# A hybrid backbone layer on one core: the third branch projection in two parts, by K tiles, with its last operands kept in SBUF

## The chip, the cores and the metric

One core of a Trainium2 chip runs the whole kernel. The metric is the device time of one execution in microseconds (us); less is better. The profile and the trace come from one further execution, recorded by the hardware profiler.

## What is computed

One layer for 256 latent tokens, with 256 context tokens as a prefix, model width 2048, all in f32:

```python
h = rms_norm(x) * (1 + scale) + shift            # latent and context tokens
(na_q, na_k, na_v, na_gate, pool_u, pool_gate, rw_r, rw_k, rw_v, rw_gate, rw_lw, rw_la, merge_logits) = split(h @ w_in)
y_na   = neighbourhood_attention(...)            # 16 heads of 64
y_pool = multiscale_pool(...)                    # windows 2, 4, 8, 16
y_rw   = rwkv_readout(wkv_scan(...), ...)        # RWKV-7, two directions, 16 heads of 64, context first
b_na, b_pool, b_rw = y_na * silu(na_gate), y_pool * silu(pool_gate), y_rw * silu(rw_gate)      # 256 x 1024 each
g_na, g_pool, g_rw = split(sigmoid(merge_logits))                                           # 256 x 2048 each
merged = g_na * (b_na @ w_branch[0]) + g_pool * (b_pool @ w_branch[1]) + g_rw * (b_rw @ w_branch[2])
out = rms_norm(x + gate * (merged @ w_out)) * final_g
```

## The kernel before, in words

**Products.** Every large product is made of f32r halves: an operand x is kept as `hi` (rounded) and `lo = x - hi`, and three matmuls (`mm3`, L582 to L584) add hi*hi, hi*lo and lo*hi. Weights come as raw tiles of 512 KB (`load_unit`, L564, three buffers `raw`); `split_half` cuts each in two halves, with a cast on ScalarE (`whi`, L576) and a subtraction on VectorE (`wlo`, L577), into five buffers of each. A *unit* is one raw tile. `group` (a product of 256 tokens by 512 columns) takes one unit for two K tiles: 4 calls of `mm3`, 12 matmuls. Two PSUM accumulators `dg`, one for each half of the tokens, come from a pool of two, so the next group's first matmul on one of them waits until `done` has read the group before.

**Stages.** Up to about 140 us the adaLN factors and h are made. Then, to about 1280 us, the columns of w_in are projected, eight head pairs of attention and of RWKV and the pooling are worked off beside them, and the 12 groups of merge logits (16 K tiles each) go to DRAM as tanh (`md_`). From 1280 us come the *branch groups*: three branches of four column groups c, 8 K tiles each, so 4 units and 48 matmuls in a group. `branch_load` (L623) fetches the operands of two K tiles at a time from DRAM (`bs`), where `keep` (L842 to L846: a cast, a subtraction and two stores) put the hi and lo halves of each head pair. K tile k of branch 2 is RWKV head pair k. `gates_in` (L923) loads a group's gates from `md_` into two buffers `mt`, which stand ahead of the last unit; `done` (L928, L930) makes (gate + 1) * accumulator on VectorE and, from branch 1 on, adds it to `sums`. After branch 2's group c, `turned` (L639 to L646) transposes the sums on TensorE and writes their hi and lo halves for w_out. From about 1479 us w_out is multiplied (L1211, L1212 split its weights).

**RWKV.** `rwkv(p)` runs for head pairs 0 to 7: features, scores, `inverse` (31 steps on VectorE and two trips through DRAM, L299 to L321), `merge`, a chain of 8 steps (`px` L374, `py` L382, `pu` L388, `pS` L398, `py` L411, each 8 small matmuls, with VectorE, ScalarE and GpSimd between them), the readout (`pm`, `pvv`, L108, L109), and `keep(2, p, g)`, after which the event `rw<p>` is marked.

**Order.** `Order` is a planner that runs when the kernel is built. It has a clock of its own (0.68 us for an `mm3` of 512 columns, given figures for the bursts of attention and RWKV and for the waits after them), and it writes TensorE's order out by hand: ready bursts of the streams go in between units. `units()` is the stream of units: first `todo`, then `late`, the twelve branch groups. A group of branch 2 is only taken when the event `rw7` lies behind on the planner's clock; three half units are taken ahead. `branch_load` 8 to 11 (branch 2's operands) too stand behind `rw7` there. From `side7` (the last attention) on, every second half unit also calls `gate_piece`: a 256 KB load `wg` (L1069) into one of the two buffers `kt`, and a VectorE instruction `gs` (L1072, L1074) that adds it up. There are 64 of these; after every 16th, `gate_out` makes a matmul `pg` and a store. All loads are issued by SyncE's queue (SP), in one order fixed at build time by the framework's scheduler, which also orders the other engines' instructions; each queue works in that order and waits where it has to. Behind the loop, SP loads x, the gate and final_g for the end (L1200, 16 loads of 256 KB).

Of the kernel before, what the change touches and what calls it, by code (L numbers as in the profile page):

```python
# [9 lines left out]
F32 = mybir.dt.float32  # L10
# [506 lines left out]
NT = 256  # L517
# [12 lines left out]
def hybrid_block(ctx, tc, x, cx, w_ms, w_st, w_in, w_mg, w_br, w_out, pool_w, icnt, wa, bias, rows, params, out, dbg=None):  # L530
# [80 lines left out]

    def branch_st(br):
        def st(k):
            c = slice(256 * (k % 2), 256 * (k % 2) + 256)
            return hh[4 * br + k // 2][:, c], hl[4 * br + k // 2][:, c]
        return st

    def branch_load(i):

        br, k = i // 4, 2 * (i % 4)  # L620
        for e, y in enumerate((hh, hl)):
            x = y[i] = hp.tile([P, 512], F32R, tag=f"h{'hl'[e]}{i}", name=f"b{'hl'[e]}{i}")
            nc.sync.dma_start(x.bitcast(F32).rearrange("p (k t) -> p k t", k=2), bs[2 * br + e][k // 2].rearrange("k p t -> p k t"))  # L623

    def branch_src(br, c):
        return lambda u: w_br[br, 4 * c:4 * c + 4, :, 256 * u:256 * u + 256].rearrange("n p c -> p n c")

    def merged(t, c):
# [3 lines left out]
        return sums[t, c]  # L632
    sums = {}
    mhl = {}
# [189 lines left out]
    with ExitStack() as mx:  # L824
# [6 lines left out]
        O = Order(tc)  # L831
        T = {}

# [82 lines left out]

        def branch_group(br, c):
            th = {}

            def gates_in(u):  # L920
                for t in range(2):
                    th[t] = wp.tile([P, 512], F32, tag="mt", bufs=2, name=f"bth{br}_{c}_{t}")
                    nc.sync.dma_start(th[t], md_[4 * br + c][t])  # L923
                return u()

            def done(t, a):
                o = merged(t, c) if br == 0 else th[t]
                nc.vector.scalar_tensor_tensor(o, th[t], 1.0, a, ALU.add, ALU.mult)  # L928
                if br:
                    nc.vector.tensor_tensor(merged(t, c), merged(t, c), o, ALU.add)  # L930
                if br == 2 and t and c < 3:
                    O.add(turn(c), 1)
            us = group(8, branch_src(br, c), branch_st(br), done)
            us[3] = lambda u=us[3]: gates_in(u)
            return us

        def turn(c):
            yield 0.0, 2.0
            for t in range(2):
                turned(c, t)  # L940
                yield 0.55, 0.2


        def rwkv(p):
# [32 lines left out]
            nc.vector.scalar_tensor_tensor(g, y, 0.5, g, ALU.mult, ALU.mult)  # L977
            keep(2, p, g)
            O.mark(f"rw{p}")

# [122 lines left out]
        for i in range(12):  # L1103
            todo.append((None, lambda i=i: merge_group(i)))
        late = [(br, c) for br in range(3) for c in range(4)]

        def units():
# [4 lines left out]
            while True:  # L1112
                while len(ready) < AHEAD:
                    if not halves:
                        if not cur:
# [3 lines left out]
                            if i is not None:  # L1119
                                cur = todo.pop(i)[1]()  # L1120
                                if not todo:
                                    last = 0
                            elif not todo and late and (late[0][0] < 2 or O.has("rw7")):
                                assert O.has("side7")
                                cur = branch_group(*late.pop(0))
                            else:
                                break
                        halves = cur.pop(0)()
                        if last is not None:
                            if last in (5, 6, 7, 8, 10, 12, 14, 16):  # L1130
                                branch_load(last - 5 if last < 9 else last // 2 - 1)
                            if last >= 18 and loads and O.has("rw7"):
                                branch_load(loads.pop(0))
                            last += 1
                    ready.append(halves.pop(0)())
                    n += 1
                    if n % 2 and O.has("side7") and gates:
                        gate_piece(*gates.pop(0))
# [144 lines left out]
```

## Time and profile before

| | us |
|---|---|
| median of 3 runs | 1576.07 (1574.93 to 1576.57) |
| the profiled execution, device time | 1578.95 |
| its span, first to last instruction | 1577.2 |
| TensorE matmul busy | 1498.5 (95%) |
| TensorE weight load | 1204.1 (76%) |
| VectorE busy | 1163.0 (74%) |
| ScalarE busy | 795.6 (50%) |
| GpSimd busy | 250.8 (16%) |

The mean granted TensorE clock is 0.985 of full speed. 289 MB move by DMA, 183 GB/s over the span. TensorE sets the length nearly everywhere; the stretch from 1275 to 1445 us is where its busy share falls.

### The profile page before, as it was taken

What the parts mean: (1) busy time and instruction counts of PE and PEld (TensorE: products, weight loads), DVE (VectorE), ACT (ScalarE), POOL (GpSimd) and SP (SyncE); (2) the same over time, 40 slices, a digit from 0 to 9 for tenths busy, and PEclk for the clock granted to TensorE, in tenths of its full rate; (3) what the DMA queues carried; (4) which work ended last, traced back from release to release, by engine and by line L of the source; (5) the groups of instructions that cost most, each with busy time, mean ns of one, the idle gap of its engine ahead of it and who ended that gap; (6) DMA issues with size and microseconds to landing.
All of it is one profiled execution on the core that took longest, in us unless ns stands there. A gap on an engine that the chain in (4) does not pass through costs nothing.

```text
span 1577.2 us, 31852 instructions
## 1 busy us (share of the span) xinstructions
PE 1498.5 (95%) x12024; PEld 1204.1 (76%) x12024; DVE 1163.0 (74%) x2630; ACT 795.6 (50%) x1593; POOL 250.8 (16%) x437
## 2 busy tenths in 40 slices
PE   6999989999999999999999999999999997987998
PEld 4667868788877897788789877877897775666887
DVE  4224787788788777886887778778779987886764
ACT  5224663566365546544664556446546542333553
POOL 2222010050023013200230230023023200120000
PEclk9999999999999999999999999999999999998999
DMA  9996435445543464343345533533566698987763
GB/s 373 343 334 229 144 128 173 145 155 176 162 142 105 131 179 142 102 131 121 98 158 153 174 96 119 165 122 113 176 191 211 209 311 246 296 261 259 242 208 112
DMA packets 210186, 289.23 MB, mean 183 GB/s; under 512 B 62576, under 2 KB 159984, under 8 KB 205424
## 3 DMA queue, kind: packets, MB, share of 16 engines
q1 hardware_dynamic: 203120, 277.76, 54.4%
q10 hardware_dynamic: 6912, 9.44, 1.7%
q8 instruction: 94, 1.54, 0.4%
q14 instruction: 60, 0.49, 0.1%
HBM read 265.38 MB, written 21.50 MB: 182 GB/s over the span
## 4 chain that ended last, share of the span: by engine, by line
PE 72%; DVE 10%; DMA 10%; ACT 3%; issue 3%; SPq 1%; ACTq 0%; POOL 0%; DVEq 0%; POOLq 0%
PE d L814 27%; PE dg L582 7%; PE dg L583 6%; PE dg L584 5%; DVE wlo L577 3%; PE acc L735 2%; PE psm L683 2%; PE o L582 2%; PE o L584 2%; PE o L583 2%; DMA raw<-in_w_br 2%; DMA raw<-in_w_in 2%; PE acc L738 2%; PE acc L741 2%; PE pu L388 1%
## 5 line engine op out<-in xcount | busy, mean ns | idle before, releaser
L576 ACT CAST whi<-raw 128x512 fp32r<-128x512 f32 x584 | 353.9, 619 | 397.7 <-PE d L814 158.9
L577 DVE TENSOR_TENSOR wlo<-raw,whi 128x512 fp32r<-128x512 f32 x584 | 401.4, 699 | 101.5 <-ACT whi L576 74.0
L814 PE MATMUL d<-hh,whi 128*128 128x256 f32 (+1 forms) x1184 | 366.4, 329 | 1.6 <-ACT mth L910 0.8
L814 PE MATMUL d<-hl,whi 128*128 128x256 f32 (+1 forms) x1184 | 357.8, 322 | 0.0
L814 PEld LDWEIGHTS d<-hh,whi 128*128 128x128 f32 x1184 | 224.8, 190 | 25.1 <-issue 2.9
L814 PE MATMUL d<-hh,wlo 128*128 128x256 f32 (+1 forms) x1184 | 241.2, 323 | 0.0
L814 PEld LDWEIGHTS d<-hl,whi 128*128 128x128 f32 x1184 | 225.2, 190 | 16.1 <-issue 0.2
L814 PEld LDWEIGHTS d<-hh,wlo 128*128 128x128 f32 x1184 | 182.4, 190 | 16.9 <-issue 0.7
L370 POOL TENSOR_SCALAR sg<-SV,G 64x64 f32<-64x64 f32 x192 | 112.4, 591 | 365.5 <-DVE SV L407 208.9
L582 PE MATMUL dg<-whi,hh 128*128 128x512 f32 x384 | 165.4, 431 | 4.9 <-DVE gnag L854 3.2
L583 PE MATMUL dg<-whi,hl 128*128 128x512 f32 x384 | 152.1, 396 | 0.0
L584 PE MATMUL dg<-wlo,hh 128*128 128x512 f32 x384 | 151.9, 396 | 0.1
L582 PE MATMUL dg<-whi,bh 128*128 128x512 f32 x192 | 82.7, 431 | 17.8 <-ACT whi L576 7.5
L582 PEld LDWEIGHTS dg<-whi,hh 128*128 128x128 f32 x384 | 73.0, 190 | 26.4 <-DVE gnag L854 4.6
L584 PEld LDWEIGHTS dg<-wlo,hh 128*128 128x128 f32 x384 | 73.0, 190 | 17.2 <-DVE wlo L577 0.6
L583 PEld LDWEIGHTS dg<-whi,hl 128*128 128x128 f32 x384 | 73.3, 191 | 10.5 <-issue 0.2
L584 PE MATMUL dg<-wlo,bh 128*128 128x512 f32 x192 | 78.4, 408 | 2.7 <-DVE wlo L577 2.7
L583 PE MATMUL dg<-whi,bl 128*128 128x512 f32 x192 | 78.0, 406 | 1.9 <-DMA bl<-bs 1.9
L309 DVE TENSOR_TENSOR iM<-iA,iT 128x126 f32<-128x126 f32 (+22 forms) x248 | 63.7, 257 | 17.1 <-DMA iA<-dA 10.8
L311 DVE TENSOR_TENSOR iT<-iT,iM 128x126 f32<-128x126 f32 (+22 forms) x248 | 62.8, 253 | 6.4
L748 ACT ACTIVATE hh<-xT,md 128x256 fp32r<-128x256 f32 x32 | 17.5, 594 | 89.3 <-DVE md L705 89.3
L582 PEld LDWEIGHTS dg<-whi,bh 128*128 128x128 f32 x192 | 37.6, 196 | 30.0 <-ACT whi L576 12.1
(320 smaller groups left out, 2510.1 us busy)
## 6 DMA issues: line engine op xcount, KB each, us to landing
raw<-in_w_in SPq DMA_DIRECT2D x244, 512.0 KB, 3.8
wm<-in_w_ms SPq DMA_DIRECT2D x32, 1024.0 KB, 6.9
raw<-in_w_br SPq DMA_DIRECT2D x48, 512.0 KB, 5.1
wg<-in_w_mg SPq DMA_DIRECT2D x64, 256.0 KB, 4.2
raw<-in_w_out SPq DMA_DIRECT2D x32, 512.0 KB, 4.2
wst<-in_w_st SPq DMA_DIRECT2D x16, 448.0 KB, 7.4
sl<-in_bias SPq DMA_DIRECT2D x32, 128.0 KB, 3.1
iA<-dA SPq DMA_DIRECT2D x16, 256.0 KB, 5.6
```

Source lines behind the costliest of these rows:

```text
L309: nc.vector.tensor_tensor(m, A[:, st:st + 1, st + 1:32].to_broadcast([128, ni, nt]), T[:, 0:ni, st:st + 1].to_broadcast([128, ni, nt]), AL ...
L311: nc.vector.tensor_tensor(T[:, 0:ni, st + 1:32], T[:, 0:ni, st + 1:32], m, ALU.add)
L370: nc.gpsimd.tensor_scalar(sg[hv[par], d], SV[hv[par], par, w, d], G[hv[par], gs[d][0], d:d + 1], None, ALU.mult)
L576: nc.scalar.copy(hi, src)
L577: nc.vector.tensor_tensor(lo, src, hi.bitcast(F32), ALU.subtract)
L582: nc.tensor.matmul(acc, a[0], b[0], start=start, stop=False)
L583: nc.tensor.matmul(acc, a[1], b[0], start=False, stop=False)
L584: nc.tensor.matmul(acc, a[0], b[1], start=False, stop=stop)
L683: mm = nc.tensor.matmul(psm[j][32 * g:32 * g + 32, 0:256], cs[:, kt], wm[:, k], start=(kt < 4), stop=(kt >= 12), tile_position=(0, 32 * g))
L735: mm = nc.tensor.matmul(acc[i], shi[:, c], hh[j], start=(j == 0), stop=False)
L738: nc.tensor.matmul(acc[i], slo[:, c], hh[j], start=False, stop=False)
L814: nc.tensor.matmul(box[0], w[m >= 8][:, 128 * i:128 * i + 128], x, start=(v == 0 and m == 0), stop=(v == 3 and m == 11))
```

## The change

The groups of branch 2 come in two parts. Part 1 of a column group takes K tiles 0 to 5 (3 units, 36 matmuls) and only needs the event `rw5`; part 2 takes K tiles 6 and 7 (1 unit, 12 matmuls) and needs `rw7`. All four groups of part 1 stand ahead of the four of part 2. Each part has its own gate multiplication and addition to `sums`; in part 2 the addition is on GpSimd for c = 0 to 2 and on VectorE for c = 3. The gates of part 2 are loaded a second time from `md_` (`ahead`), during part 1 for c = 0 to 2, into buffers `kt`, `sl` and `vT`, which `gate_piece` and `gate_out` used until then, and for c = 3 into the two buffers `mt`, with its unit. So that those buffers are free, a gate piece comes with two of three half units instead of one of two. Head pair 7 is not stored and loaded again: its two halves stay in SBUF (`T["last"]`). `branch_load` 8 to 11 need `rw6` instead of `rw7`, come with every second unit, and the last one loads only head pair 6. The planner waits 3.0 us instead of 2.0 before the transposes.

```diff
--- before.py
+++ after.py
@@ -609,8 +609,11 @@
             return [lambda h=h: half(h) for h in range(2)]
         return [lambda u=u: load(u) for u in range(nk // 2)]
 
-    def branch_st(br):
+    def branch_st(br, k0=0):
         def st(k):
+            k += k0
+            if br == 2 and k == 7:
+                return T["last"]
             c = slice(256 * (k % 2), 256 * (k % 2) + 256)
             return hh[4 * br + k // 2][:, c], hl[4 * br + k // 2][:, c]
         return st
@@ -620,17 +623,21 @@
         br, k = i // 4, 2 * (i % 4)
         for e, y in enumerate((hh, hl)):
             x = y[i] = hp.tile([P, 512], F32R, tag=f"h{'hl'[e]}{i}", name=f"b{'hl'[e]}{i}")
+            if i == 11:
+                nc.sync.dma_start(x[:, 0:NT].bitcast(F32), bs[2 * br + e][3][0])
+                continue
             nc.sync.dma_start(x.bitcast(F32).rearrange("p (k t) -> p k t", k=2), bs[2 * br + e][k // 2].rearrange("k p t -> p k t"))
 
-    def branch_src(br, c):
-        return lambda u: w_br[br, 4 * c:4 * c + 4, :, 256 * u:256 * u + 256].rearrange("n p c -> p n c")
+    def branch_src(br, c, u0=0):
+        return lambda u: w_br[br, 4 * c:4 * c + 4, :, 256 * (u + u0):256 * (u + u0) + 256].rearrange("n p c -> p n c")
 
     def merged(t, c):
 
         if (t, c) not in sums:
             sums[t, c] = hp.tile([P, 512], F32, tag=f"h{'hl'[t]}{12 + c}", name=f"sum{t}_{c}")
         return sums[t, c]
-    sums = {}
+    sums, T = {}, {}
+
     mhl = {}
 
     def turned(c, t):
@@ -829,7 +836,6 @@
         hps = cp.tile([P, 8], F32, name="hps")
         nc.vector.tensor_scalar(hps, pp[:, PC_PS:PC_PS + 8], 0.5, None, ALU.mult)
         O = Order(tc)
-        T = {}
 
         def ztile(tag, nm, n):
             z = zp.tile([P, n, 258], F32, tag=tag, bufs=1, name=nm)
@@ -914,7 +920,8 @@
             src = lambda u: w_in[MERGE + 4 * i:MERGE + 4 * i + 4, :, 256 * u:256 * u + 256].rearrange("n p c -> p n c")
             return group(16, src, lambda k: (hh[k][:, 256:512], hl[k][:, 256:512]), lambda t, d: merge_out(i, t, d))
 
-        def branch_group(br, c):
+        def branch_group(br, c, part=0):
+
             th = {}
 
             def gates_in(u):
@@ -923,19 +930,38 @@
                     nc.sync.dma_start(th[t], md_[4 * br + c][t])
                 return u()
 
+            def ahead(u):
+
+                for t in range(2):
+                    tag, n = (("kt", 2), ("sl", 3), (("sl", 3), ("vT", 1))[t], ("mt", 2))[c]
+                    pool = wp if tag == "mt" else np_
+                    x = gates2[c, t] = pool.tile([P, 512], F32, tag=tag, bufs=n, name=f"cth{c}_{t}")
+                    nc.sync.dma_start(x, md_[8 + c][t])
+                return u()
+
             def done(t, a):
-                o = merged(t, c) if br == 0 else th[t]
-                nc.vector.scalar_tensor_tensor(o, th[t], 1.0, a, ALU.add, ALU.mult)
+                g = gates2[c, t] if part == 2 else th[t]
+                o = merged(t, c) if br == 0 else g
+                nc.vector.scalar_tensor_tensor(o, g, 1.0, a, ALU.add, ALU.mult)
                 if br:
-                    nc.vector.tensor_tensor(merged(t, c), merged(t, c), o, ALU.add)
-                if br == 2 and t and c < 3:
+                    (nc.gpsimd if part == 2 and c < 3 else nc.vector).tensor_tensor(merged(t, c), merged(t, c), o, ALU.add)
+                if part == 2 and t and c < 3:
                     O.add(turn(c), 1)
-            us = group(8, branch_src(br, c), branch_st(br), done)
-            us[3] = lambda u=us[3]: gates_in(u)
+            if part == 2:
+                us = group(2, branch_src(br, c, 3), branch_st(br, 6), done)
+                if c == 3:
+                    us[0] = lambda u=us[0]: ahead(u)
+                return us
+            us = group(6 if part else 8, branch_src(br, c), branch_st(br), done)
+            us[-1] = lambda u=us[-1]: gates_in(u)
+            if part and c < 3:
+                us[1] = lambda u=us[1]: ahead(u)
             return us
 
+        gates2 = {}
+
         def turn(c):
-            yield 0.0, 2.0
+            yield 0.0, 3.0
             for t in range(2):
                 turned(c, t)
                 yield 0.55, 0.2
@@ -975,8 +1001,15 @@
             yield f"rwg{p}"
             g = T[f"rwg{p}"]
             nc.vector.scalar_tensor_tensor(g, y, 0.5, g, ALU.mult, ALU.mult)
-            keep(2, p, g)
-            O.mark(f"rw{p}")
+            if p < 7:
+                keep(2, p, g)
+            else:
+                h = wp.tile([P, NT], F32R, tag="th", bufs=1, name="lasth")
+                l = np_.tile([P, NT], F32R, tag="ql", name="lastl")
+                nc.scalar.copy(h, g)
+                nc.vector.tensor_tensor(l, g, h.bitcast(F32), ALU.subtract)
+                T["last"] = h, l
+            O.mark(f"rw{p}", 1.5 * (p == 7))
 
         def attention(p):
             yield f"nav{p}"
@@ -1102,7 +1135,7 @@
                     todo.append((f"at{p}", gate_(PL_G + p - 1 + e, f"plg{p - 1 + e}", "g2p", 2)))
         for i in range(12):
             todo.append((None, lambda i=i: merge_group(i)))
-        late = [(br, c) for br in range(3) for c in range(4)]
+        late = [(br, c) for br in range(2) for c in range(4)] + [(2, c, part) for part in (1, 2) for c in range(4)]
 
         def units():
             ready, halves, cur = [], [], []
@@ -1120,7 +1153,7 @@
                                 cur = todo.pop(i)[1]()
                                 if not todo:
                                     last = 0
-                            elif not todo and late and (late[0][0] < 2 or O.has("rw7")):
+                            elif not todo and late and (len(late[0]) < 3 or O.has(("rw5", "rw7")[late[0][2] - 1])):
                                 assert O.has("side7")
                                 cur = branch_group(*late.pop(0))
                             else:
@@ -1129,12 +1162,12 @@
                         if last is not None:
                             if last in (5, 6, 7, 8, 10, 12, 14, 16):
                                 branch_load(last - 5 if last < 9 else last // 2 - 1)
-                            if last >= 18 and loads and O.has("rw7"):
+                            if last >= 18 and last % 2 == 0 and loads and O.has("rw6"):
                                 branch_load(loads.pop(0))
                             last += 1
                     ready.append(halves.pop(0)())
                     n += 1
-                    if n % 2 and O.has("side7") and gates:
+                    if n % 3 and O.has("side7") and gates:
                         gate_piece(*gates.pop(0))
                 if not ready:
                     if not todo and not late:
```

## Rows read from the trace of the kernel before

**Rows 1.** Page, 40 slices of the span: TensorE's busy share, tenths.
```profile
PE   6999989999999999999999999999999997987998
```

**Rows 2.** Stretches: us, busy PE, PEld, DVE, ACT, POOL, PEclk, DMA share, GB/s.
```profile
1230.00:1240.00 10.00, 9.94 (x82) 7.41 (x82) 9.87 (x20) 7.70 (x21) 3.72 (x7) 1.00 0.51 158
...
1290.00:1300.00 10.00, 8.06 (x27) 5.89 (x26) 8.58 (x21) 2.35 (x5) 0.00 (x0) 0.83 1.03 351
...
1330.00:1340.00 10.00, 5.26 (x24) 4.06 (x23) 3.48 (x8) 0.83 (x2) 0.00 (x0) 1.00 0.66 176
...
1410.00:1420.00 10.00, 5.80 (x45) 4.08 (x42) 6.71 (x19) 3.24 (x6) 0.00 (x0) 0.59 0.55 179
...
1430.00:1440.00 10.00, 2.72 (x6) 1.86 (x7) 1.16 (x2) 0.00 (x0) 0.00 (x0) 0.62 0.93 306
...
1450.00:1460.00 10.00, 10.00 (x47) 7.95 (x47) 8.24 (x15) 5.04 (x10) 0.00 (x0) 1.00 1.00 342
```

**Rows 3.** Timeline of TensorE, 1407 to 1443 us: start, duration, instruction, [idle before].
```profile
1407.61 0.40 PE L584 MATMUL dg<-wlo,bh 128*128 128x512 f32 x1
...
1418.93 0.63 PE L582 MATMUL dg<-whi,bh 128*128 128x512 f32 x1
...
1428.15 0.39 PE L583 MATMUL dg<-whi,bl 128*128 128x512 f32 x1
1428.38 0.39 PE L584 MATMUL dg<-wlo,bh 128*128 128x512 f32 x1
1435.41 0.77 PE L582 MATMUL dg<-whi,bh 128*128 128x512 f32 x1 [6.64 <-DMA bh<-bs]
...
1442.77 0.39 PE L582 MATMUL dg<-whi,bh 128*128 128x512 f32 x1
```

**Rows 4.** Chain that ended last, 1428 to 1438 us: start, duration, what.
```profile
1428.17 3.41 DMA bs<-kh
...
1432.07 5.93 DMA bl<-bs
```

**Rows 5.** Timeline of TensorE, chain bursts with units beside them.
```profile
1402.70 0.45 PE L398 MATMUL pS<-SV,BKT 128*64 128x64 f32 x8
...
1403.46 0.50 PE L582 MATMUL dg<-whi,bh 128*128 128x512 f32 x1
```

**Rows 6.** Timeline of SP: the first and the last of the 64 gate-piece loads.
```profile
1175.05 0.41 SPq L1069 DMA_DIRECT2D wg<-in_w_mg  x1
...
1425.41 0.33 SPq L1069 DMA_DIRECT2D wg<-in_w_mg  x1
```

**Rows 7.** Chain that ended last, 1287 to 1300 us.
```profile
1287.22 4.49 DMA wg<-in_w_mg
1291.73 0.76 DVE gs L1074
...
1292.95 6.88 DMA raw<-in_w_br
```

**Rows 8.** Groups of 1441 to 1492 us: busy us, mean ns, idle before.
```profile
L577 DVE TENSOR_TENSOR wlo<-raw,whi 128x512 fp32r<-128x512 f32 x21 | 14.4, 688 | 5.4 <-ACT whi L576 4.7 <-PE mt L639 0.3
...
L928 DVE SCALAR_TENSOR_TENSOR bth<-bth,dg 128x512 f32<-128x512 f32 x8 | 5.5, 686 | 10.4 <-PE dg L584 10.4
L646 DVE SCALAR_TENSOR_TENSOR ml<-mt,mh 128x256 fp32r<-128x256 f32 x12 | 4.8, 416 | 0.3 <-ACT mh L645 0.3
```

**Rows 9.** Timeline of TensorE: the first matmul behind two group ends.
```profile
1294.14 0.50 PE L582 MATMUL dg<-whi,bh 128*128 128x512 f32 x1 [1.94 <-DVE sum L928]
...
1481.20 0.50 PE L582 MATMUL o<-wh,mh 128*128 128x512 f32 x1 [0.33 <-DVE bth L928]
```

**Rows 10.** Groups of GpSimd over the span: the largest addition with two inputs.
```profile
L754 POOL TENSOR_TENSOR slo<-wst,shi 128x896 fp32r<-128x896 f32 x16 | 33.9, 2116 | 102.6 <-ACT shi L753 96.9 <-DMA wst<-in_w_st 5.6
```

**Rows 11.** Timelines of VectorE and of GpSimd, 1198 to 1200 us.
```profile
1198.54 0.90 DVE L577 TENSOR_TENSOR wlo<-raw,whi 128x512 fp32r<-128x512 f32 x1
...
1198.85 1.06 POOL L93 TENSOR_TENSOR t1k<-zk 128x256 f32<-128x256 f32 x1
```

## The prediction, made before the changed kernel was run

> **What bounds the kernel now.** I read the slices of the page first: TensorE is at 9 tenths or more nearly everywhere, and its longest weak spell lies in the last fifth [rows 1]. The table of stretches splits this in two. From about 1280 to 1350 us TensorE lacks weights: it is busy 8.06 of 10 us at 1290 while the DMA engines are full (351 GB/s), and 5.26 of 10 us at 1330. From 1410 to 1440 us it has nothing it may do: 5.80 and 2.72 of 10 us, with a granted clock of 0.59 and 0.62 [rows 2]. The timeline shows that second hole. Branch 1's last matmul starts at 1407.61, branch 2's first at 1418.93; its 36 matmuls on K tiles 0 to 5 end behind 1428.38; K tile 6 starts at 1435.41 after waiting for a load, and the group's 12 matmuls on K tiles 6 and 7 end at 1442.77 [rows 3]. The chain of waits names the road of that load: a store of 3.41 us, then a load of 5.93 us, both for head pair 7 [rows 4].
>
> **What the hole costs.** At full clock a matmul follows the one before by 0.23 us (1428.15 to 1428.38 [rows 3]).
> - First gap: 1407.61 + 0.23 = 1407.84 to 1418.93, 11.1 us. It holds TensorE work that stays: seven bursts of 8 small matmuls and four of 256 columns. Beside units, two bursts (pS, then py) take 1403.46 - 1402.70 = 0.76 us, 0.38 each [rows 5]; the 256-column matmuls I take at half of 0.23. 7 x 0.38 + 4 x 0.12 = 3.1, so 8.0 us go.
> - Slow restart: 1418.93 to 1428.38 + 0.23 is 9.7 us; 36 x 0.23 = 8.3. So 1.4 us go.
> - Second gap and restart: 1428.61 to 1442.77 is 14.2 us for 12 matmuls, 2.8 us of work. So 11.4 us go.
>
> Together 20.8 us, if the changed order fills the hole. It can: part 1 is 4 x 36 = 144 matmuls x 0.23 = 33.1 us. Behind 1407.84 stand 3.1 us of bursts and these 33.1, so part 2 starts near 1444. Head pair 7 is ready soon after the chain's 1428.17, where its store began [rows 4], and is now used from SBUF: some 15 us to spare. The store and the load of head pair 7 go too, which is worth nothing beyond that, since they are what the second gap waited for. On the planner's clock it fits as well: what is left of chain and readout when units run out sums to 27.3 us of its figures plus the mark's 1.5, against 48 calls x 0.68 = 32.6 us and the bursts.
>
> **What comes in.** TensorE's matmuls stay the same in number. Three tolls:
>
> *Gate pieces earlier.* The 64 loads run from 1175.05 to 1425.41, 250 us [rows 6], one of two half units. At two of three they need three quarters of the half units: 188 us, 2.93 us a piece instead of 3.91. A quarter, 16 pieces, moves to where branch 0 and the merges run. There VectorE is busy 9.87 of 10 us at 1230 [rows 2] and each piece costs it 0.76 us [rows 7]: 12 us of work more. They bring 4.2 MB, and the operand loads 8 to 11 come into the stretch too (1.8 MB): 6.0 MB at 351 GB/s is 17 us. Behind each `wg` on SP stand the raw tiles, and the two `kt` buffers turn in 4.49 + 0.76 us, 5.29 from issue to issue [rows 7], 2.65 a piece: just enough for 2.93. Bounds: 0 (all hidden: the DMA moves only 158 and 176 GB/s at 1230 and 1330 [rows 2]) to 17 us. What leaves the time after 1363 gives nothing back there, for TensorE is full then. I take 5.5, a third, because slack is there but not in every stretch.
>
> *Part 2 is short.* A group of it gives TensorE 12 x 0.23 = 2.8 us and about 0.7 of transposes. VectorE has two `wlo` (0.688 each), two gate multiplications (0.686) and four `ml` (0.416) [rows 8]: 4.4 us. It falls behind by 0.9 us a group, 3.8 in all, against a stock of five split halves (3.4 us). There are also four more group ends at which TensorE waits for an accumulator; two such waits took 1.94 and 0.33 us [rows 9], so 1.3 to 7.8 us for four. I take 2.5, near the lower end, which is from the same part of the kernel. The six additions on GpSimd take 2.116 x 512/896 = 1.2 us each by the nearest row [rows 10], inside the 3.0 us that the planner leaves before the transposes; I cost them at nothing while that holds. Without it, a transpose waits and the next group with it.
>
> Such an addition also meets VectorE: `wlo` took 0.90 us beside GpSimd's work on two inputs [rows 11], 0.688 as a mean [rows 8]. By these rows 0.21 us a meeting; two meetings for each of six additions are 2.5 us of VectorE at the worst, within the bounds above. The Trainium skill (SBUF — State Buffer, Who interferes with whom) says it harder: a VectorE instruction with two SBUF inputs and a GpSimd one that reads SBUF exclude each other for a whole instruction. By that rule the toll is what the fourth rival below gives; the row shows a delay, but of only part of an instruction.
>
> *Denser DMA after 1408.* From 1407.84 to the start of w_out's second accumulator, 1481.20 [rows 9], there were 73.4 us; without the hole 52.6. In them lie 16 raw tiles (8.4 MB) and 16 gate loads (4.2 MB, half of them new): 240 GB/s. The 16 loads for the end, another 4.2 MB, lift that to 319 if they come as early as now; the stretches show 342 with TensorE full and 351 with it starved [rows 2]. Bounds 0 and 4.2 MB at 345 GB/s, 12 us. I take 2.0, since these loads are needed only after the first quarter of w_out. Part 2's gates for c = 3 are loaded in its own unit; if late, VectorE waits, and w_out's first accumulator behind it; that is in this term.
>
> **Sum.** -20.8 + 5.5 + 2.5 + 2.0 = -10.8 us. The profiled execution took 1578.95 us (span 1577.2), 2.9 above the median of 1576.07; so 1568.2 by its own time, and **1565.3** against the median. Some 0.2% (3.2 us) is what a measurement of this kernel can tell from no change.
>
> **Rivals.**
> 1. *The tolls hide.* The pieces fit into the DMA's slack and into waits that VectorE has anyway, and only 0 to 3 us come back: 1555.3 to 1558, say 1557. For: 2.65 is under 2.93. Against: 9.87 of 10 us. Chance 0.20.
> 2. *Slower: the gate ring blocks SP.* Between 1175 and 1363 SP waits at `wg` for a `kt` buffer, and the raw tiles stand behind. It binds when the two buffers turn in over 2 x 2.93 = 5.9 us, and decides the sign when the loss passes 16.3 us (20.8 less the other tolls): 16.3/64 = 0.25 us a piece, a turn of 6.4 us, so a landing of 5.6 instead of 4.49. A raw tile landed in 6.88 in the same spell [rows 7]. At a landing of 5.85 the turn is 6.6, the loss 64 x 0.375 = 24 us: 1576.1 - 20.8 + 4.5 + 24 = 1583.8. Chance 0.10.
> 3. *No change.* DMA throughput takes its whole bound of 17 us: -20.8 + 17 + 4.5 = +0.7, 1576.8. Chance 0.10.
> 4. *GpSimd's additions shut VectorE out*, 6 x 1.2 = 7.3 us more: 3.8 + 7.3 - 3.4 = 7.7 instead of 2.5, so 1570.5. Chance 0.06, since no row shows so long a block.
> 5. *It doesn't do what it says*: `rw7` comes after part 1's units on the planner's clock, and a hole of some 5 us stays: 1570.3. Chance 0.04.
>
> The forecast has 0.50, with a range of its own of 1560 to 1571. **How the numbers follow.** The range 1556 to 1577 leaves out rival 2 and the lower end of rival 1. Faster: 0.50 + 0.20 + 0.06 + 0.04 = 0.80; within 0.2%: 0.10; slower: 0.10.
>
> **What would show it.** Right: no wait of TensorE for `bh` or `bl` near the end, granted clock 1.00 in every stretch after its chain's end, part 1 running beside the last chain steps and the readout, the last `wg` near 1363 to 1375, w_out's second accumulator starting near 1470. The first toll shows as lower TensorE shares between 1175 and 1365 and `px` of head pair 7 starting later; the second as waits for L928 at part 2's ends; the third as raw landings over 6 us after 1410. Wrong: the hole still there (rival 5), or the time from 1175 to 1408 grown by over 16 us (rivals 2 and 3).

## The result, and the profile of the changed kernel

| us | before | changed |
|---|---|---|
| median of 4 runs each, same chip | 1575.5 (1573.67 to 1576.57) | 1586.3 (1582.16 to 1587.59) |
| the profiled execution, device time | 1578.95 | 1585.6 |
| its span | 1577.2 | 1583.9 |

The changed kernel is slower: the ratio is 1.0065, with a 95% interval of 1.0044 to 1.0087, some 10 us. The forecast was 1565.3, and the range of 1556 to 1577 did not hold the time. The two profiled executions are only 6.7 us apart, since that of before lies above all four of its runs; some 4 us of the difference can therefore not be placed in the account by landmarks below.

The page of the changed kernel, TensorE's share in 40 slices, against [rows 1]:

```profile
PE   6999989999999999999999999999999886899898
```

The weak slice of before, the 7 behind the 98 near the end, is gone. Four slices further ahead fell in its place, from 9979 to 8868. The table of stretches shows the same in us (columns as in [rows 2]):

```profile
1290.00:1300.00 10.00, 5.59 (x19) 3.79 (x19) 8.00 (x26) 2.25 (x4) 0.00 (x0) 0.76 0.97 325
1410.00:1420.00 10.00, 10.00 (x80) 7.22 (x79) 7.24 (x16) 3.82 (x9) 2.88 (x5) 1.00 0.71 211
1430.00:1440.00 10.00, 10.00 (x80) 7.39 (x80) 6.97 (x19) 4.16 (x8) 0.00 (x0) 1.00 0.53 173
1470.00:1480.00 10.00, 5.38 (x29) 3.80 (x27) 10.00 (x14) 5.23 (x11) 6.16 (x4) 0.98 0.80 284
```

Where TensorE was busy 5.80 and 2.72 of 10 us [rows 2], it is now busy without a break and at the full granted clock. But at 1290 it has 5.59 where it had 8.06, and a new weak place stands at 1470, where VectorE is busy 10.00 of 10 us. The timeline of TensorE shows the hole closed, against [rows 3]:

```profile
1427.18 0.40 PE L584 MATMUL dg<-wlo,bh 128*128 128x512 f32 x1
1427.51 0.45 PE L388 MATMUL pu<-xs,AT 64*64 64x64 f32 x8
1427.89 0.50 PE L582 MATMUL dg<-whi,bh 128*128 128x512 f32 x1
...
1465.79 0.40 PE L582 MATMUL dg<-whi,lasth 128*128 128x512 f32 x1
```

Branch 1's last matmul and part 1's first are one burst apart (0.71 us, 11.32 before), and the first matmul on head pair 7, from SBUF, waits for nothing. Yet 1427.18 stands where 1407.61 stood.

**An account by landmarks.** Both kernels have 576 branch matmuls, so the start of the k-th one can be compared. The second column is the start in the changed kernel less that in the kernel before.

| landmark | before, us | lag of the changed kernel, us |
|---|---|---|
| first branch matmul | 1279.83 | +4.1 |
| the 193rd (branch 1 begins) | 1346.38 | +15.7 |
| the 384th (branch 1's last) | 1407.61 | +19.6 |
| the 528th (part 2 is next) | 1467.05 | -2.2 |
| first matmul of w_out | 1479.08 | +7.0 |
| end of the span | 1577.2 | +6.7 |

So the change lost 19.6 us before 1427, won 21.8 us over the hole, lost 9.2 us around part 2, and w_out's own stretch is as long as before. Of the second and the third number 1.4 us are a shift: four bursts of transposes (0.35 us each, from one burst's start to the next matmul's) lay ahead of the 528th matmul before and lie behind it now. Without them the hole gave 20.4 us and part 2 cost 7.8.

Stages of the changed kernel, and then the first two of the kernel before:

```profile
1175.00:1265.00 90.00, 83.39 (x766) 62.38 (x765) 79.38 (x167) 51.67 (x110) 21.66 (x36) 1.00 0.71 227
1265.00:1365.00 100.00, 79.83 (x410) 57.69 (x409) 77.73 (x164) 32.86 (x56) 0.00 (x0) 0.87 0.91 284
1410.00:1465.00 55.00, 54.76 (x340) 41.66 (x339) 42.81 (x84) 25.59 (x48) 5.00 (x9) 1.00 0.64 206
1465.00:1486.00 21.00, 16.15 (x73) 12.18 (x72) 19.61 (x30) 10.03 (x22) 8.94 (x6) 0.92 0.80 263
```

```profile
1175.00:1265.00 90.00, 86.57 (x793) 65.31 (x792) 79.77 (x169) 54.88 (x116) 23.79 (x36) 0.98 0.68 220
1265.00:1365.00 100.00, 83.80 (x520) 61.69 (x518) 79.92 (x174) 35.65 (x61) 1.85 (x4) 0.97 0.89 283
```

From 1265 to 1365 the records hold 410 matmuls of TensorE where they held 520, at a granted clock of 0.87 instead of 0.97. The DMA moved 284 GB/s instead of 283: no more bytes went through in that stretch, though more pieces were asked for. What went through shows in the DMA issues there, first of the kernel before and then of the changed one:

```profile
raw<-in_w_br SPq DMA_DIRECT2D x24, 512.0 KB, 6.0
wg<-in_w_mg SPq DMA_DIRECT2D x25, 256.0 KB, 4.5
```

```profile
raw<-in_w_br SPq DMA_DIRECT2D x19, 512.0 KB, 5.6
wg<-in_w_mg SPq DMA_DIRECT2D x29, 256.0 KB, 4.7
bl<-bs SPq DMA_DIRECT2D x9, 256.0 KB, 5.7
bh<-bs SPq DMA_DIRECT2D x8, 256.0 KB, 5.8
```

Four pieces more went through, and five operand loads more (17 of 256 KB instead of 12), while five raw tiles, which TensorE lives on, stayed behind. The queue of SP shows how. Its timeline, and then the part of VectorE's timeline that it waits for:

```profile
1300.46 0.39 SPq L564 DMA_DIRECT2D raw<-in_w_br  x1
1304.27 0.34 SPq L1102 DMA_DIRECT2D wg<-in_w_mg  x1
...
1307.03 0.34 SPq L1102 DMA_DIRECT2D wg<-in_w_mg  x1
...
1308.36 0.43 SPq L564 DMA_DIRECT2D raw<-in_w_br  x1
1309.42 0.33 SPq L1102 DMA_DIRECT2D wg<-in_w_mg  x1
...
1312.97 5.07 SPq L1102 DMA_DIRECT2D wg<-in_w_mg  x2
1318.13 0.94 SPq L564 DMA_DIRECT2D raw<-in_w_br  x2
```

```profile
1312.19 0.75 DVE L1107 SCALAR_TENSOR_TENSOR gs<-wg,cs,gs 128x512 f32<-128x512 f32 x1 [1.33 <-DMA wg<-in_w_mg]
1312.86 0.28 DVE L309 TENSOR_TENSOR iM<-iA,iT 128x128 f32<-128x128 f32 x1
...
1316.12 0.28 DVE L309 TENSOR_TENSOR iM<-iA,iT 128x121 f32<-128x121 f32 x1
1316.32 0.68 DVE L577 TENSOR_TENSOR wlo<-raw,whi 128x512 fp32r<-128x512 f32 x1
1316.92 0.75 DVE L1107 SCALAR_TENSOR_TENSOR gs<-wg,cs,gs 128x512 f32<-128x512 f32 x1
```

The chain of waits has the piece issued at 1307.03:

```profile
1307.03 5.14 DMA wg<-in_w_mg
```

It lands after 5.14 us and is added up at 1312.19, and its buffer is issued again at 1312.97: a turn of 5.94 us, where the prediction read 5.29. The piece of 1309.42 lands after 6.29 us, at 1315.71, and is added up at 1316.92, when eleven steps of `inverse` and a split half are done; so its buffer turns in over 8 us, of which 1.2 are the late sum. SP stands at that second `wg` until then, and two raw tiles stand behind it until 1318.13; they came just in time. The wait that TensorE shows here belongs to an earlier tile:

```profile
1315.82 0.80 PE L582 MATMUL dg<-whi,bh 128*128 128x512 f32 x1 [3.56 <-ACT whi L576]
```

That tile was issued at 1308.36 and landed at 1315.05. Between it and the tile of 1300.46 lie a stand of SP at `wg` (until 1304.27, for the sum that frees the buffer), two operand loads, another piece and two gate loads. Over the whole spell, from 1174 to branch 1's last matmul, the view of SP's waits has 90.2 us in all at `wg` where it had 67.4 before, and 48.0 at raw tiles where it had 58.4: part of the waiting only moved.

The waits of TensorE from 1174 to 1500 (us in total, times, longest):

```profile
PE dg L582 <- ACT whi L576: 10.7, 4, 3.6
PE pg L1092 <- DVE gs L1107: 6.2, 1, 6.2
PE dg L584 <- DVE wlo L577: 4.7, 4, 3.0
PE mt L646 <- DVE ml L653: 3.8, 2, 2.2
PE dg L582 <- DVE bth L945: 3.7, 3, 2.4
```

Before, the same view had 7.5 us for `whi`, 6.6 for `bh`, 1.9 for `bl` and 1.3 for `pg`. The waits for `bh` and `bl` are gone; the waits for `whi` and `pg`, and in part 2 for `ml`, are longer.

### The profile page after: what moved, and what is told of

Its sections match the earlier page's. It is cut to its first block, busy times and chain, and to the rows that moved or that the text cites. A ratio compares the mean times of both kernels' runs of the same rounds, so it can differ in the third digit from the quotient of the medians.

```text
span 1583.9 us, 31861 instructions
## 1 busy us (share of the span) xinstructions
PE 1503.0 (95%) x12024; PEld 1204.8 (76%) x12024; DVE 1174.0 (74%) x2640; ACT 794.7 (50%) x1593; POOL 256.4 (16%) x443
## 4 chain that ended last, share of the span: by engine, by line
PE 70%; DVE 13%; DMA 10%; issue 3%; ACT 2%; SPq 1%; POOL 0%; ACTq 0%; DVEq 0%; POOLq 0%
PE d L821 28%; PE dg L582 6%; PE dg L583 5%; PE dg L584 5%; DVE wlo L577 3%; DMA wg<-in_w_mg 3%; PE acc L742 2%; PE psm L690 2%; DMA raw<-in_w_br 2%; PE o L584 2%; PE o L583 2%; PE o L582 2%; PE acc L745 2%; PE acc L748 2%; DMA iA<-dA 1%
## 5 line engine op out<-in xcount | busy, mean ns | idle before, releaser
L755 ACT ACTIVATE hh<-xT,md 128x256 fp32r<-128x256 f32 x32 | 17.5, 594 | 89.3 <-DVE md L712 89.3
```

## The experiments

The theory at this point: the pace of the gate pieces is the loss ahead of 1427, through the two `kt` buffers and SP's order; the rest lies in part 2, where GpSimd's additions slow VectorE. The rivals: the loss comes from the denser DMA traffic as such, or from the VectorE work that the pieces bring. Ratios are to the kernel before, run in the same series (its median there: 1574.27 for the first four runs, 1573.01 for the next four, 1574.81 for the three after that, 1573.92 for the last two).

**The pace alone**, in the kernel before:

```diff
-                    if n % 2 and O.has("side7") and gates:
+                    if n % 3 and O.has("side7") and gates:
```

> The kernel before with one edit: a gate piece comes with two of three half units instead of one of two. Theory (the faster pieces are the first toll): branch 1 ends 15 to 20 us later than before and the time is 12 to 20 us longer, about 1590, with the hole behind branch 1 as wide as before. Rival (the operand loads 8 to 11, moved ahead, or something else of the change made that lag): branch 1 ends at most 4 us later and the time stays within 4 us of before.

Measured: 1592.06, ratio 1.0122 [1.0092, 1.0151]. Branch 1's last matmul starts at 1423.52, 15.9 us later than before, and the hole is as wide (to 1434.32, 10.8 us against 11.3). This one figure costs 18 us by the medians and 19 by the ratio, without any other part of the change.

**The additions of part 2 on VectorE**, in the changed kernel:

```diff
-                    (nc.gpsimd if part == 2 and c < 3 else nc.vector).tensor_tensor(...)
+                    nc.vector.tensor_tensor(...)
```

> The changed kernel with all additions of part 2 on VectorE, none on GpSimd. Theory (the GpSimd additions hold up VectorE's two-input instructions and so part 2): 4 to 6 us less than the changed kernel, about 1581, with the wlo and wl rows of part 2 back at 0.7 us. Rival (part 2 is slow because VectorE simply has too much to do in it): no gain, or up to 2 us more, since VectorE gets 6 x 0.68 = 4.1 us of additions more.

Measured: 1584.72, ratio 1.0059 [1.0038, 1.0080], against 1.0065 for the changed kernel: no gain that the intervals show. The rows say why. VectorE's timeline of the changed kernel, and GpSimd's beside it:

```profile
1468.93 3.14 DVE L577 TENSOR_TENSOR wlo<-raw,whi 128x512 fp32r<-128x512 f32 x2
...
1473.20 0.68 DVE L945 SCALAR_TENSOR_TENSOR cth<-cth,dg 128x512 f32<-128x512 f32 x1
1473.80 1.18 DVE L577 TENSOR_TENSOR wlo<-raw,whi 128x512 fp32r<-128x512 f32 x1
...
1475.23 1.42 DVE L1245 TENSOR_TENSOR wl<-raw,wh 128x512 fp32r<-128x512 f32 x1
...
1477.84 1.65 DVE L1245 TENSOR_TENSOR wl<-raw,wh 128x512 fp32r<-128x512 f32 x1
...
1480.08 1.28 DVE L1245 TENSOR_TENSOR wl<-raw,wh 128x512 fp32r<-128x512 f32 x2
```

```profile
1468.53 3.00 POOL L947 TENSOR_TENSOR sum<-sum,cth 128x512 f32<-128x512 f32 x2 [43.71 <-DVE cth L945]
1472.75 3.35 POOL L947 TENSOR_TENSOR sum<-sum,cth 128x512 f32<-128x512 f32 x2 [1.23 <-DVE cth L945]
1477.66 1.28 POOL L947 TENSOR_TENSOR sum<-sum,cth 128x512 f32<-128x512 f32 x1 [1.56 <-DVE cth L945]
```

Two `wlo` beside two additions take 3.14 us, 1.57 each, where the two `wl` of 1480.08, beside none, take 0.64 each. Five subtractions meet an addition: 3.14 + 1.18 + 1.42 + 1.65 = 7.4 us, against 3.4 at 0.69 for a `wlo` and 0.64 for a `wl`, so VectorE loses 4.0 us. In the single records each of the five ends 0.54 to 0.56 us behind the end of the addition that it met: it waits the addition out. The six additions on VectorE instead are 6 x 0.68 = 4.1 us. It is an even exchange.

**Part 2's gates in buffers of their own, with the old pace.** The gates go where operands of earlier branches stood, so no buffer of the pieces has to be free for them:

```diff
-                    tag, n = (("kt", 2), ("sl", 3), (("sl", 3), ("vT", 1))[t], ("mt", 2))[c]
-                    pool = wp if tag == "mt" else np_
-                    x = gates2[c, t] = pool.tile([P, 512], F32, tag=tag, bufs=n, ...)
+                    x = gates2[c, t] = hp.tile([P, 512], F32, tag=f"h{'hl'[t]}{2 * c}", ...)
...
-                if c == 3:
-                    us[0] = lambda u=us[0]: ahead(u)
...
-            if part and c < 3:
+            if part:
                 us[1] = lambda u=us[1]: ahead(u)
...
-                    if n % 3 and O.has("side7") and gates:
+                    if n % 2 and O.has("side7") and gates:
```

> The changed kernel, but the gates of part 2 are loaded into buffers of their own (those that held branch 0's and branch 1's operands), and the gate pieces come with one of two half units again. Theory (faster pieces are the first toll): branch 1 ends within 5 us of before, and the time falls by 13 to 19 us against the changed kernel, to about 1570, under the kernel before. Rival (the operand loads ahead made the lag): branch 1 still ends 10 us or more later than before, and the time stays above 1580.

Measured: 1570.52 over 10 runs, ratio 0.9980 [0.9966, 0.9994]. Branch 1's last matmul starts at 1410.54, 2.9 us later than before instead of 19.6. In 1265 to 1365 this kernel issues 24 raw tiles and 24 pieces, as the kernel before did with one more piece. It still has 17 operand loads of 256 KB there, so those are not the loss; at most they are in the 2.9 us.

**The same with the additions on VectorE**:

> The run before it with all additions of part 2 on VectorE as well. Both theories together: 4 to 6 us under that run, about 1565. If VectorE's amount of work is what part 2 lacks, the same time as that run or up to 2 us more.

Measured: 1568.18, ratio 0.9967 [0.9954, 0.9979]. The 2.3 us against the run before it are less than was expected, and the intervals overlap. The even exchange stands. VectorE's timeline at the start of part 2, first of the run before, with the additions on GpSimd, then of this one:

```profile
1455.39 3.18 DVE L577 TENSOR_TENSOR wlo<-raw,whi 128x512 fp32r<-128x512 f32 x2
```

```profile
1453.54 1.28 DVE L577 TENSOR_TENSOR wlo<-raw,whi 128x512 fp32r<-128x512 f32 x2
```

**Own buffers, and the new pace**, so that these two runs differ by the pace alone (`n % 3` again in the kernel with own buffers):

> e3_own_buffers with the gate pieces again at two of three half units: the pace is the one difference between the two. Theory (the pace makes the first toll): 13 to 18 us over e3, about 1586, and branch 1 ends 15 us or more later than in e3. Rival (in the changed kernel it was the sharing of the buffers kt, sl and vT with part 2's gates): within 3 us of e3.

Measured: 1582.32, ratio 1.0067 [1.0046, 1.0087]. Against 0.9980 the pace is worth 0.0087, 13.7 us. And against the changed kernel's 1.0065 the place of the gates is worth nothing. The loss is the pace; the next runs ask through what it acts.

**Three buffers for the pieces at the new pace**: every third piece goes into `vT`, which only `gate_out` uses then.

```diff
-            wg = np_.tile([P, 512], F32, tag="kt", bufs=2, ...)
+            tag, nb = ("vT", 1) if kt % 3 == 2 else ("kt", 2)
+            wg = np_.tile([P, 512], F32, tag=tag, bufs=nb, ...)
```

> e5 with a third buffer for the gate pieces (every third piece goes into vT, whose other user is gate_out). Ring theory (the two kt buffers turn too slowly and SP waits at wg with the raw tiles behind): 8 us or more under e5. Rival (VectorE's work for the pieces, or the bytes, set the pace): within 3 us of e5.

Measured: 1575.4, ratio 1.0019 [0.9998, 1.0041]: 0.0048 back, 7.5 us, half of the loss. (Of this run and the next the profiled execution lies at the long end of the runs, so their landmarks are not set against the medians.)

**Two buffers, but the sum on 64 of the 512 columns.** The loads stay whole; most of the output gate's sum is left out, and `gs` becomes short:

```diff
-  ...scalar_tensor_tensor(gs[cc], wg, cs[:, kt, 1:2], gs[cc], ALU.mult, ALU.add)
+  ...scalar_tensor_tensor(gs[cc][:, 0:64], wg[:, 0:64], cs[:, kt, 1:2], gs[cc][:, 0:64], ALU.mult, ALU.add)
```

> e5 with the VectorE instruction of each piece but the first of 16 cut to 64 of its 512 columns, so most of the output gate's sum is left out; the loads stay whole. VectorE theory: VectorE has some 60 x 0.55 = 33 us less to do up to branch 1's end, and the time falls 12 us or more under e5, to about 1573 or less. Ring theory: the turn of two buffers shortens from 5.3 to 4.7 us, a gain of 2 to 6 us. DMA theory (the bytes): within 2 us of e5.

Measured: 1575.38, ratio 1.0011 [0.9988, 1.0034]: 0.0056 back, 8.8 us. It lies between what the ring theory expected (2 to 6 us) and what the VectorE theory did (12 or more), so it doesn't decide between them: a shorter sum also frees its buffer sooner.

**Only three groups split, and the transposes later.** Group c = 3 of branch 2 stays whole and stands between part 1 and part 2 of the others; the transposes of c = 0 to 2 go into the start of w_out, which takes K tiles 12 to 15 first. The additions are on VectorE and the pace is the old one:

```diff
-late = ... + [(2, c, part) for part in (1, 2) for c in range(4)]
+late = ... + [(2, 0, 1), (2, 1, 1), (2, 2, 1), (2, 3, 1), (2, 0, 2), (2, 1, 2), (2, 2, 2)]
...
-            us = group(6 if part else 8, branch_src(br, c), branch_st(br), done)
+            us = group(6 if part and c < 3 else 8, branch_src(br, c), branch_st(br), done)
...
+    uo = (6, 7, 0, 1, 2, 3, 4, 5)
```

> e4_own_buffers_vector with only c = 0 to 2 of branch 2 in two parts; c = 3 runs whole (8 K tiles) between the parts 1 and the parts 2, and the transposes of c = 0 to 2 move into the start of w_out, which takes its K tiles in the order 12 to 15, 0 to 11. VectorE loses two multiplications and two additions, and the transposes no longer lie between short groups. Theory (part 2 is short of VectorE): 3 to 6 us under e4, about 1564, the fastest so far, with no wait of TensorE for ml. Rival (the ends of the short groups cost what they cost wherever the transposes are): within 1.5 us of e4.

Measured: 1567.35, ratio 0.9970 [0.9952, 0.9988], no different from 0.9967. w_out begins 4.2 us earlier (1463.82 against 1468.00) and the span is as long (1566.3 against 1566.1): w_out's stretch, which now holds the transposes, is 4.4 us longer.

**The pieces late instead of early**, in that kernel: one of three half units in the first 20 branch units, then two of three.

```diff
-                    if n % 2 and O.has("side7") and gates:
+                    if (n % 2 if last is None or last < 9 else n % 3 == 0 if last < 29 else n % 3) and O.has("side7") and gates:
```

> e8_three_short_groups with another pace of the gate pieces: one of two half units until the branch groups begin, one of three in the first 20 units of them, two of three behind that. Theory (between 1265 and 1365 us the DMA engines are full, and each piece there takes the place of half a raw tile): some 7 pieces, 1.8 MB, leave that stretch, at 290 GB/s 6 us; branch 1 ends 3 to 7 us earlier than in e8 and the time falls by as much, to about 1562. Rival (the inverse and SP's waits set that stretch, not the bytes): within 1.5 us of e8.

Measured: 1570.02, ratio 0.9970 [0.9956, 0.9983], no gain. In 1265 to 1365 it issues 25 raw tiles and 20 pieces, and at the 145th branch matmul it is 5.6 us ahead of the kernel it was made from; at the 337th the lead is gone (1.8 us behind).

**Half the bytes at the new pace.** Loads and sums cover 256 of the 512 columns of a piece; half of the output gate's sum is left out (set to zero, and the first piece of 16 is cut likewise, not shown):

```diff
-nc.sync.dma_start(wg, w_mg[cc, kt // 2, :, kt % 2])
+nc.sync.dma_start(wg[:, 0:256], w_mg[cc, kt // 2, :, kt % 2, 0:256])
...
-  ...scalar_tensor_tensor(gs[cc], wg, cs[:, kt, 1:2], gs[cc], ALU.mult, ALU.add)
+  ...scalar_tensor_tensor(gs[cc][:, 0:256], wg[:, 0:256], cs[:, kt, 1:2], gs[cc][:, 0:256], ALU.mult, ALU.add)
```

> e5_own_buffers_fast_pieces with each piece cut to half of its columns, load and sum alike, so that half of the output gate's sum is left out: half of the bytes, and an instruction of VectorE of about 0.42 us instead of 0.75. Bytes theory: 64 x 128 KB = 8.4 MB less, and the time falls clearly under e7, which had cut VectorE's work further and kept the bytes: 1570 or less. VectorE theory: less gain than e7, so 1577 or more.

Measured: 1572.31, ratio 0.9991 [0.9974, 1.0008]. That is 0.0076 better than with whole pieces, 12 us; but it shortens the load, the sum and the bytes together, so alone it doesn't say which.

**Three buffers and short sums together**, with whole loads (the sum again on 64 columns):

> e6 and e7 together: fast pieces, three buffers, and sums cut to 64 columns (most of the output gate's sum left out), with whole loads. If the ring and VectorE are two causes beside each other, their two gains of 7 us add up and the time is that of e3, about 1570. If both only shorten the same turn and the rest is bytes, it stays within 2 us of e6 and e7, about 1575.

Measured: 1571.73, ratio 0.9981 [0.9963, 0.9998], where the old pace has 0.9980. Two changes that leave every byte in place give back as much as the pace took. The stretch of 1265 to 1365 of this kernel, and its DMA issues in it:

```profile
1265.00:1365.00 100.00, 82.30 (x501) 60.57 (x499) 68.12 (x173) 32.98 (x58) 1.38 (x3) 0.91 0.95 306
```

```profile
raw<-in_w_br SPq DMA_DIRECT2D x22, 512.0 KB, 6.1
wg<-in_w_mg SPq DMA_DIRECT2D x30, 256.0 KB, 5.3
```

The DMA moves 306 GB/s where the kernel that it was made from moved 284 in this stretch, with one piece and one raw tile more (against the changed kernel, three raw tiles). There was room for the bytes; the queue did not get to them. SP's waits at `wg` from 1174 to branch 1's last matmul sum to 58.5 us here, against 89.6 with own buffers at the new pace and 71.7 at the old one. So the two changes do more to the ring than undo the pace; what they would give at the old pace wasn't run, and that they return just the loss of the pace isn't shown. That no byte had to go is.

**The closing matmul later**, at the new pace with two buffers: the row of waits with the largest single entry was `pg` for `gs`, so the planner is told to leave 20 us ahead of `pg`.

```diff
-            yield 0.0, 2.0
+            yield 0.0, 20.0
```

> e5_own_buffers_fast_pieces with the matmul pg that closes 16 pieces put 20 us behind the last piece on the planner's clock instead of 2. Theory (with fast pieces the planner's place for pg comes before its pieces have landed and been summed, and TensorE stands at pg, 8.0 us in e5's profile): the waits of pg for gs fall under 2 us and the time 4 to 8 us, to about 1576. Rival (pg only shows a shortage that the next wlo or whi would show): within 2 us of e5, with longer waits for whi and wlo.

Measured: 1583.0, ratio 1.0058 [1.0039, 1.0077], against 1.0067. TensorE's waits from 1174 to 1410 without this edit, and with it:

```profile
PE dg L582 <- ACT whi L576: 8.2, 5, 3.0
PE pg L1088 <- DVE gs L1103: 8.0, 1, 8.0
```

```profile
PE dg L582 <- ACT whi L576: 16.5, 6, 5.6
```

The wait of 8.0 us is gone, and the waits for `whi`, so for raw tiles, have grown by 8.3. This profiled execution took 1589.22 us, 6 above its median, so a part of the 8.3 may be its own; that the time stayed is in the ratios. `pg` was where the lateness showed, not what made it.

**The best arrangement**: three split groups, the old pace, the additions on VectorE, and 10 us ahead of `pg`.

> e8_three_short_groups with pg 10 us behind its pieces instead of 2: its profile has 3.4 us of waits of TensorE at pg. Theory: 1.5 to 3.5 us under e8, by the ratios to the kernel before. Rival (the shortage shows elsewhere): within 1.5 us of e8.

Measured: 1567.93 over 12 runs (1561.76 to 1570.3), ratio 0.9957 [0.9942, 0.9972], 6.8 us below the kernel before and 17 below the changed one. Its step over the arrangement with 2 us ahead of `pg` (0.9970) lies within the intervals.

## Why the prediction was wrong

**The hole: right.** 20.8 us were to go; the landmarks give 20.4. That it is so near is in part luck, as the last paragraph of this section shows. The mechanism is as told: no wait for `bh` or `bl`, clock 1.00 from 1410 to 1465, TensorE busy 54.76 of those 55 us. The spare time was overrated: head pair 7 was ready 5 us ahead of its use and not 15, as VectorE's timeline shows beside the matmul of 1465.79:

```profile
1460.78 0.42 DVE L1010 TENSOR_TENSOR lastl<-grwg,lasth 128x256 fp32r<-128x256 f32 x1
```

The text put part 1 behind the chain's bursts; the planner ran the two side by side, which filled the hole as well.

**Gate pieces earlier: the step that failed.** It took 5.5 us between bounds of 0 and 17; the lag is 19.6, the pace alone is 13.7 (own buffers) to 19 (in the kernel before). Two things were wrong in it. First, its upper bound was made of bytes over DMA throughput, and bytes are not what limits here: with all of them in place, three buffers and short sums bring the time back to that of the old pace. Second, "2.65 a piece: just enough for 2.93" had the turn of two buffers from one row [rows 7], and left 0.28 us a piece for everything that makes a turn longer, in a stage where it had itself read VectorE at 9.87 of 10 us. That row was a short one, and the trace of before showed it: of the 25 pieces that it issued from 1265 to 1365, five were landed and added up within 5.3 us of their issue, and the mean was 6.8 us. With two buffers that is 3.4 us a piece, which fits the old pace of 3.91 and not the new one of 2.93. Landings of 5.14 and 6.29 us, and a sum behind `inverse`, made the turns of 5.94 and over 8 us. The mark that the text set itself shows it too: the last piece was to be issued near 1363 to 1375. SP's timeline has

```profile
1174.37 0.90 SPq L1102 DMA_DIRECT2D wg<-in_w_mg  x2
...
1391.05 1.61 SPq L1102 DMA_DIRECT2D wg<-in_w_mg  x2
```

which is 217 us for 64 pieces, 3.4 each instead of 2.93. (The pieces come with the units, so these rows show the lag and not what made it.)

**Rival 2 was what happened, in half.** "The gate ring blocks SP" had the place, the sign and nearly the time (1583.8 against 1586.3), at a chance of 0.10. Its price came from longer landings alone. A third buffer gives 7.5 us of 13.7, so about half of the loss goes with the size of the ring. Shorter sums give 8.8, both 13.5. What the sums take beside the ring, by the work on VectorE that the text counted ("12 us of work more") and then hid, stays open: a later `gs` that holds the buffer and a later `wlo` that holds TensorE were not told apart.

**Rival 3 fell.** It had DMA throughput take 17 us. With every byte in place the DMA moved 306 GB/s where the changed kernel moved 284, and later pieces brought no gain.

**Part 2 is short: right in kind, 2.5 instead of 7.8 us**, at the very end of its bounds of 1.3 to 7.8. VectorE is the busiest engine there, 19.61 of 21.00 us. The text had it 3.8 us behind against a stock of 3.4. The additions on GpSimd, costed at nothing, cost VectorE 4.0 us: 3.8 + 4.0 - 3.4 = 4.4. The rest up to 7.8 is in the ends of the groups (TensorE's waits for `bth` and `cth`) and in a granted clock of 0.92; how it divides was not settled. **Rival 4** named that block, with 7.3 us. The rule it stood beside, of the Trainium skill (SBUF — State Buffer, Who interferes with whom), was borne out where the row of before [rows 11] showed only a delay in part: `wlo`, with two inputs in SBUF, went from 0.64 to 1.57 us beside an addition, and the additions themselves from 1.28 to 1.50 (3.00 for two). The gate multiplication of 1473.20, with one input in PSUM, kept its 0.68 beside an addition, as the same section of the Trainium skill has it for one SBUF input. But the rule did not decide the time, since the additions on VectorE cost as much.

**Denser DMA after 1408: nothing instead of 2.0 us.** From w_out's first matmul to the end of the span it is 97.8 us, against 98.1 before.

**Sum.** Forecast: -20.8 + 5.5 + 2.5 + 2.0 = -10.8. By landmarks: -20.4 + 19.6 + 7.8 - 0.3 = +6.7. Of the 17.5 us between them, 14.1 are the first toll and 5.3 the second, less 1.9 for the other two. (The medians are 10.8 us apart; the 4 us more are in no landmark, as said above.) **Rivals 1 and 5** fall with it: the tolls did not hide, and no hole stayed.

**What stays open.** With the old pace and own buffers, hole and part 2 would give 12.6 us by these numbers; the two runs of that kind show 3.2 and 5.2. In the profile with own buffers and GpSimd's additions the landmarks, without the shift, give +2.9 ahead of the hole, -17.2 for it, and +8.7 around part 2. So the hole gives 3 us less there. With own buffers and the new pace it gives some 20 us again, and the pace is all that differs. At the old pace the last piece is issued at 1434.77, inside the filled hole, where VectorE is busy 45.63 of the 50 us from 1407 to 1457 and TensorE waits for `whi`, `bth` and `pg`. The prediction had it that pieces moved away from there give nothing back; these rows speak against that, but no run took it apart from the earlier end of branch 1.

## What to carry to other kernels

An edit that moves work forward only to have a buffer free has to be priced at the queue which that work stands in: with two buffers and an issuing queue that works in order, compare the pace with all the turns that the trace shows in the busy stage, from issue to the end of the consumer, and not with one short turn. A cheaper way can be another buffer for the moved data; here buffers of their own for the gates let the pieces keep the old pace, and that turned the loss into a gain. And the longest wait in the table can be only the place at which lateness shows: when one 8.0 us wait was taken away, the time stayed and the waits for weights grew.

## What the runs showed of the hardware

- Beside a GpSimd addition of 128x512 with both inputs in SBUF, a VectorE subtraction of the same size with both inputs in SBUF takes 1.57 us instead of 0.64 (two of them 3.14), ending 0.54 to 0.56 us behind the addition's end, and one of VectorE's multiplications with an input in PSUM stays at 0.68.
- Moving six such additions from GpSimd to VectorE (6 x 0.68 us) frees about as much (4.0 us) as it costs, so that in neither pair of kernels the runs tell the two places apart.
- In the weight-starved stretch from 1265 to 1365 us the DMA engines moved 306 GB/s in one kernel (busy share 0.95) where they moved 284 in the changed one (0.91): that share did not mean that the bytes were the limit.
